# Six channel tiles of a gated convolution in pairs, seven block products in place of eight, and the latent q and k of two heads side by side

## The chip, the cores and the metric

The kernel runs on one core of one Trainium2 chip. The time is the device time of one execution in microseconds; before the change its median over three runs is 1995.36 us (1992.71 to 1997.35).

## What is computed

Two layers of a hybrid block over 256 context rows and 1024 latent rows of width 1024, all in float32. The change is in the first layer's input projection; its outputs are:

```
p = h @ w_in                                  # h: 1280 rows x 1024
q, k, v, g_a, a_f, a_b, c_b, c_c, c_x, g_b = split(p)
# 4 heads of gated linear attention: q, k 128 wide, v 256 wide, chunks of 64 rows, both directions
b = cumsum(log_gate)                          # per chunk
scores = (q * exp(b)) @ (k * exp(-b)).T       # masked; o = scores @ v + q_in @ state
o = rmsnorm(o_f + o_b) * silu(g_a)            # g_a: 8 tiles of 128 channels
# 8 channel tiles of 128 of the short convolution
z = c_c * c_x
y = c_b * conv3(z) * silu(g_b)                # conv3 within grid rows of 64 latents, or within the context
x = x + gate * (concat(o, y) @ w_out)
```

The second layer is a gated linear recurrence over 16 blocks of 128 channels with its own projections, and a final norm follows.

## The kernel before, in words

**Products.** h stands transposed in SBUF, 8 row blocks (k) of 128 by 1280 columns, as a high and a low float32r part (`hhi`, `hlo`). A weight unit of 128 output channels is two loads of 128x512 (`load_unit`, L115); each load goes through `load_split` (L104): a DMA into one of two `raw` buffers, a cast to the high part on ScalarE (L111), a subtraction for the low part on VectorE (L112) into one of six `hl` buffers. `mm3` (L123) makes one product of three matmuls (L125 to L127), and `proj` (L144) runs 8 of them for each column chunk of `CH`: 256 context columns and twice 512 latent columns. A unit is so 24 matmuls of 256 columns and 48 of 512.

**Stages.** A start stage norms h and projects q and k of head 0. Then for each of four heads: `emit_gla(h)` (L527), two gate units (L560, L562), four batches of `presplit` (L165), one convolution tile (`emit_conv`, L195, four units: cc, cx, cb and a gate), and q, k, v of the next head. `presplit` loads 128x512 weights of the second layer, splits them and stores both parts in DRAM for later. Behind the heads come convolution tiles 4 to 7, the modulation vectors (`mod`, L576: 32 loads of 512 KB and 56 reductions on VectorE, L586), the first output projection, the recurrence blocks and the last output projection.

**What sets the order.** From the heads to the first output projection the instructions are put in order by a scheduler, which takes the program's order as priority and fills each engine when an instruction's inputs are ready by its own timeline; the recurrence has a fixed order. Each engine runs its list in that order. Buffers bound it: two `raw`, six `hl`, and in PSUM three banks of tag A (projections), three of tag G (attention) and two of tag B (transposes).

**The attention's chain.** For one chunk `emit_gate` (L405) makes a matmul `pz` (L411), from it ScalarE and VectorE make the gate b (L414 to L420, a scan at the end), `emit_factors` (L423) makes from b, q and k the factors `qh`, `kh` (L456, L459), and `emit_scores` (L477) multiplies these: `psc` (L484 on). A chunk is called by head, direction (1 backward, 0 forward) and first column: `pz2_0_0` is head 2, forward, context. The buffers of q and k are one per chunk (L231), so the next head's projection can be copied out of PSUM when the factors of the present head are made.

## Time and profile before

| | |
|---|---|
| median of 3 runs | 1995.36 us |
| profiled execution, its own time | 2002.68 us |
| span of its trace | 2000.9 us |
| TensorE matmul (PE) busy | 1932.0 us, 97% |
| TensorE weight load (PEld) busy | 1588.5 us, 79% |
| VectorE (DVE) busy | 1317.8 us, 66% |
| ScalarE (ACT) busy | 961.3 us, 48% |

The profiled execution is 7.3 us over the median, 1.8 us of its time lie outside the span. Matmuls are pipelined, so that the busy time of one is longer than the distance from its start to the next start; the distance is what it costs. The heads run from about 120 to 830 us of the span, the convolution tiles 4 to 7 to about 990 us.

### The profile page before, as it was taken

The page shows a single profiled execution, that of the slowest core. Times are in us where ns is not written, and L with a number is a line of the kernel's source. Part 1 is how long each engine was busy: PE and PEld are TensorE (multiplying, and loading weights), DVE is VectorE, ACT ScalarE, POOL GpSimd, SP SyncE. Part 2 cuts the span into 40 slices and gives each one's busy share as a digit, 9 for nine tenths or more (in the row PEclk, how much of TensorE's full clock was granted, in tenths as well). Part 3 has the DMA queues.
Part 4 walks back from the last instruction along what each step waited for, and adds up shares of the span by engine and source line. Part 5 has one row for each costly group of instructions (what it writes and reads, how often), then busy time and mean ns, then how long its engine had stood idle before and what let it go on. Part 6 is the DMA issues. An engine that isn't in the chain of part 4 may idle for free.

```text
span 2000.9 us, 27096 instructions
## 1 busy us (share of the span) xinstructions
PE 1932.0 (97%) x9884; PEld 1588.5 (79%) x9884; DVE 1317.8 (66%) x2103; ACT 961.3 (48%) x1690; POOL 105.2 (5%) x154
## 2 busy tenths in 40 slices
PE   9899999999999999999999899999999999998988
PEld 5777898888788888888776678878888888876767
DVE  6746436543552554388557474689999999996595
ACT  4333344334433433311345444267777776876452
POOL 1000000000000000000000000201111010100000
PEclk9999999999999999999999999999999999999999
DMA  9256217514721751366655665434333343324782
GB/s 357 82 195 199 78 50 252 175 43 146 244 89 33 245 192 53 124 223 197 205 175 178 209 222 173 139 111 127 120 118 120 115 121 121 116 81 156 264 290 88
DMA packets 162522, 311.45 MB, mean 156 GB/s; under 512 B 16338, under 2 KB 37202, under 8 KB 162260
## 3 DMA queue, kind: packets, MB, share of 16 engines
q1 hardware_dynamic: 140628, 267.78, 40.1%
q0 software_dynamic: 21760, 41.95, 7.5%
q8 instruction: 77, 1.26, 0.3%
q14 instruction: 57, 0.47, 0.1%
HBM read 221.05 MB, written 88.60 MB: 155 GB/s over the span
## 4 chain that ended last, share of the span: by engine, by line
PE 60%; DMA 19%; DVE 12%; ACT 5%; issue 4%; SPq 1%; POOL 0%; DVEq 0%; ACTq 0%; POOLq 0%
PE pjgt L126 4%; PE pjgt L127 4%; PE pjgt L125 4%; DMA rawpre<-in_w1f 4%; PE pjxr L125 4%; PE pjxr L127 4%; PE pjxr L126 4%; PE pO L126 3%; PE pO L125 3%; PE pO L127 3%; PE po L515 2%; DMA wt<-in_wmT 2%; DMA rawo<-in_w0out 2%; PE pv L125 2%; PE pv L126 2%
## 5 line engine op out<-in xcount | busy, mean ns | idle before, releaser
L125 PE MATMUL pjgt<-hhi,wgt 128*128 128x512 f32 (+1 forms) x640 | 240.6, 376 | 6.0 <-DVE zc L218 6.0
L125 PE MATMUL pO<-wo,yh 128*128 128x512 f32 x576 | 224.2, 405 | 17.6 <-ACT wo L111 16.6
L126 PE MATMUL pjgt<-hlo,wgt 128*128 128x512 f32 (+1 forms) x640 | 240.5, 376 | 0.0
L127 PE MATMUL pjgt<-hhi,wgt 128*128 128x512 f32 (+1 forms) x640 | 239.5, 376 | 0.0
L126 PE MATMUL pO<-wo,yh 128*128 128x512 f32 x576 | 231.1, 402 | 7.2 <-DVE wo L112 7.2
L127 PE MATMUL pO<-wo,yl 128*128 128x512 f32 x576 | 228.5, 399 | 0.0
L806 DVE SCALAR_TENSOR_TENSOR xc<-xp,col,xc 128x1283 f32<-128x1283 f32 (+2 forms) x102 | 149.8, 1476 | 3.2
L111 ACT CAST wo<-rawo 128x512 fp32r<-128x512 f32 x160 | 98.0, 619 | 110.7 <-DMA rawo<-in_w0out 74.9
L112 DVE TENSOR_TENSOR wo<-rawo,wo 128x512 fp32r<-128x512 f32 x160 | 108.5, 687 | 63.6 <-ACT wo L111 63.0
L125 PEld LDWEIGHTS pO<-wo,yh 128*128 128x128 f32 x576 | 109.3, 191 | 50.0 <-ACT wo L111 22.5
L125 PEld LDWEIGHTS pjgt<-hhi,wgt 128*128 128x128 f32 x640 | 121.0, 189 | 30.1 <-DVE zc L218 6.6
L126 PEld LDWEIGHTS pjgt<-hlo,wgt 128*128 128x128 f32 x640 | 121.1, 189 | 23.7 <-issue 1.1
L127 PEld LDWEIGHTS pjgt<-hhi,wgt 128*128 128x128 f32 x640 | 120.5, 189 | 23.4 <-issue 0.7
L126 PEld LDWEIGHTS pO<-wo,yh 128*128 128x128 f32 x576 | 109.7, 190 | 36.8 <-DVE wo L112 12.4
L125 PE MATMUL pjxr<-hhi,wxr 128*128 128x512 f32 (+1 forms) x384 | 137.4, 359 | 0.0
L126 PE MATMUL pjxr<-hlo,wxr 128*128 128x512 f32 (+1 forms) x384 | 137.1, 358 | 0.0
L127 PE MATMUL pjxr<-hhi,wxr 128*128 128x512 f32 (+1 forms) x384 | 136.8, 358 | 0.0
L127 PEld LDWEIGHTS pO<-wo,yl 128*128 128x128 f32 x576 | 109.8, 191 | 24.6 <-DVE yl L685 0.3
L112 DVE TENSOR_TENSOR wpre<-rawpre,wpre 128x512 fp32r<-128x512 f32 x80 | 55.1, 690 | 90.1 <-ACT wpre L111 89.7
L125 PE MATMUL pv<-wv,hhi 128*128 128x256 f32 (+1 forms) x320 | 91.8, 287 | 2.4 <-ACT v L387 2.4
L127 PE MATMUL pv<-wv,hlo 128*128 128x256 f32 (+1 forms) x320 | 92.9, 290 | 0.0
L126 PE MATMUL pv<-wv,hhi 128*128 128x256 f32 (+1 forms) x320 | 92.8, 290 | 0.0
(270 smaller groups left out, 4527.9 us busy)
## 6 DMA issues: line engine op xcount, KB each, us to landing
w1s_d<-wpre SPq DMA_DIRECT2D x160, 256.0 KB, 2.6
rawo<-in_w0out SPq DMA_DIRECT2D x96, 256.0 KB, 3.2
rawpre<-in_w1f SPq DMA_DIRECT2D x64, 256.0 KB, 3.1
wt<-in_wmT SPq DMA_DIRECT2D x32, 512.0 KB, 4.3
rawo<-in_w1out SPq DMA_DIRECT2D x64, 256.0 KB, 3.3
wxr<-w1s_d POOLq DMA_DIRECT2D x32, 512.0 KB, 3.8
wgt<-w1s_d POOLq DMA_DIRECT2D x32, 512.0 KB, 3.8
wm<-in_wmT SPq DMA_DIRECT2D x24, 512.0 KB, 8.1
```

The costliest lines, as they stand in the source:

```text
L111: S.copy(hi, raw)
L112: V.tensor_tensor(lo, raw, hi.bitcast(F32), ALU.subtract)
L125: PE.matmul(ps, a[0], b[0], start=first, stop=False)
L126: PE.matmul(ps, a[0], b[1], start=False, stop=False)
L127: PE.matmul(ps, a[1], b[0], start=False, stop=last)
L515: PE.matmul(ps[:, :DV], l, r, start=(i == 0), stop=(i == len(pairs) - 1))
L806: V.scalar_tensor_tensor(x, tap(j), cw[j], x, op0=ALU.mult, op1=ALU.add)
```

## The change

The latents of convolution tiles 0, 1, 2, 4, 5, 6 leave the loop over heads and the plain tiles; they are computed in three pairs (0, 4), (1, 5), (2, 6), each quantity (cc, cx, cb, gate) of a pair by seven products of half blocks. A pair of units is a 256 x 1024 weight block A (halves of the channels by halves of k) against h as halves of k by halves of the latents; sums and differences of the blocks of h are made once (`make_t`), those of A for each job (`pair`), and seven products of 4 `mm3` of 512 columns stand for eight. The context columns of all eight tiles stay in the loop over heads, two tiles a head, and the split parts of the paired tiles' weights are stored in DRAM there. Tiles 3 and 7 stay plain. h is held in a context tile `hC` and a latent tile `hL`. q and k of the next head move right behind `emit_gla(h)`; odd heads have their own buffers for latent q and for the last latent k chunk.

```diff
+    hC = [hpool.tile([P, KD, NCTX], F32R, name=f"hC{i}") for i in range(2)]
+    hL = [hpool.tile([P, KD, NLAT], F32R, name=f"hL{i}") for i in range(2)]
...
+            if i < len(save) and save[i] is not None:
+                for j, part in enumerate((hi, lo)):
+                    SY.dma_start(save[i][:, j], part.bitcast(F32))
...
         def new_qk(kind, d, h, c0, n):
-            t = ap.tile([P, n], F32, tag=f"{kind}{c0}", name=f"{kind}{h}_{c0}")
+            pool = odd[0] if h % 2 and (kind, c0) != ("k", 256) and c0 else ap
+            t = pool.tile([P, n], F32, tag=f"{kind}{c0}", name=f"{kind}{h}_{c0}")
...
             for h in range(H):
                 emit_gla(h)
-                emit_raw_gate(w0f[8 + 2 * h], 2 * h)
-                presplit(5)
-                emit_raw_gate(w0f[9 + 2 * h], 2 * h + 1)
-                presplit(5)
-                for _ in emit_conv(h):
+                if h + 1 < H:
+                    emit_qk(h + 1)
+                for i in (2 * h, 2 * h + 1):
+                    emit_raw_gate(8 + i, i)
+                    presplit(5)
+                    run(emit_conv(i, CH[0]))
                     presplit(5)
                 if h + 1 < H:
-                    emit_qk(h + 1)
                     emit_v(h + 1)
-    for ct in range(H, KD - 1):
-        run(emit_conv(ct))
-    run(emit_conv(KD - 1, CH[:2]))
+    def make_t(tp):
...
+        for k in range(4):
+            def raw(kk, c0):
...
+                V.tensor_tensor(r, hi.bitcast(F32), lo.bitcast(F32), ALU.add)
+                return r
+            b11, b12, b22, b21 = raw(k, 256), raw(k, 768), raw(4 + k, 768), raw(4 + k, 256)
+            V.tensor_tensor(b11, b12, b11, ALU.subtract)
+            V.tensor_tensor(b12, b22, b12, ALU.subtract)
+            V.tensor_tensor(b22, b22, b11, ALU.subtract)
+            V.tensor_tensor(b21, b21, b22, ALU.subtract)
...
+                S.copy(dst[0], r)
+                V.tensor_tensor(dst[1], r, dst[0].bitcast(F32), ALU.subtract)
...
+    def pair(tp, T, units, nm, put):
...
+        a11 = saved(0, 0)
+        r11, r21, r22, r12 = raw(0, 0), raw(1, 0), raw(1, 1), raw(0, 1)
+        p = product("A", a11, block(0, 256))
+        S.copy(x1, p)
+        V.tensor_tensor(r21, r11, r21, ALU.subtract)
+        V.tensor_tensor(r22, r22, r21, ALU.subtract)
+        s2 = parts(r22, "s2")
+        a12 = saved(0, 1)
+        p = product("A", s2, comb(2))
...
+        put(0, 0, product("G", a12, block(4, 256)), x1, x1)
+        s3 = parts(r21, "s3")
+        p5 = product("G", s1, comb(1))
...
+        put(0, 1, product("G", s4, block(4, 768)), u4, u4)
...
+    run(emit_conv(3, CH[2]))
+    T_ = make_t(tp)
+    for ct in (3, KD - 1):
+        run(emit_conv(ct, CH[1]))
...
+    for units, nm, put, around in jobs:
...
+        pair(tp, T_, units, nm, put)
...
+    rest = emit_conv(KD - 1, CH[2], "B")
```

How the order changes is shown at three places. The first is TensorE at the forward context chunk of head 2. Before, `pz2_0_0` stands within a convolution product (`pjcx2`), and 83 other matmuls follow before its scores `psc2_0_0`; the rows are those around `pz2_0_0`.

```order
L125 MATMUL pjcx2_768_5663<-hhi_84,wcx2_0_1_5608 128x512
L126 MATMUL pjcx2_768_5663<-hlo_85,wcx2_0_1_5608 128x512
L411 MATMUL pz2_0_0_4876<-aT_843,wst_837 128x256
L127 MATMUL pjcx2_768_5663<-hhi_84,wcx2_0_1_5608 128x512
L125 MATMUL pjcx2_768_5663<-hhi_84,wcx2_0_1_5608 128x512
L126 MATMUL pjcx2_768_5663<-hlo_85,wcx2_0_1_5608 128x512
```

Of the changed kernel, the same engine and chunk:

```order
L527 MATMUL pst2_1_5_4790<-v2_5_4500,k1T2_1_256_4772 128x256
L527 MATMUL pst2_1_4_4794<-v2_4_4473,k1T2_1_256_4772 128x256
L527 MATMUL pst2_1_3_4798<-v2_3_4446,k1T2_1_256_4772 128x256
L434 MATMUL pz2_0_0_4804<-aT_847,wst_841 128x256
L507 MATMUL psc2_0_0_4843<-qh2_0_0_4823,kh2_0_0_4824 64x128
L508 MATMUL psc2_0_0_4843<-qh2_0_0_4823,kh2_0_0_4824 64x64
L507 MATMUL psc2_0_0_4843<-qh2_0_0_4823,kh2_0_0_4824 64x128
L508 MATMUL psc2_0_0_4843<-qh2_0_0_4823,kh2_0_0_4824 64x64
L128 MATMUL pjgt4_0_5373<-hC0_84,wgt4_0_0_5365 128x256
```

The scores now stand right behind `pz2_0_0`, and the next projection (`pjgt4`, a gate unit) behind the scores. The four heads read alike here.

The second place is VectorE at the weights of the next head's v. Before, the splits `wv3` (L112) stand beside the forward chunks of head 2:

```order
L495 COPY_PREDICATED Cs_844<-msk_76,psc2_0_0_4915 64x256
L496 COPY_PREDICATED Cs_844<-msk_76,psc2_0_0_4915 64x2x64
L498 COPY_PREDICATED Ds_846<-msk_76,psc2_0_0_4915 64x2x64 x2
L499 TENSOR_TENSOR Cs_844<-Cs_844,Ds_846 128x256
L88 TENSOR_SCALAR rvo2_0_4931<-sso2_0_4929 128x1
L88 TENSOR_SCALAR rvo2_1_4952<-sso2_1_4950 128x1
L509 SCALAR_TENSOR_TENSOR S0_2_1_4965<-S0_2_0_4944,dec2_0_0_4890,pst2_0_1_4963 128x256
L415 TENSOR_SCALAR b2_2_0_256_4968<-pz2_0_256_4969,col_74 128x512
L112 TENSOR_TENSOR wv3_0_6131<-rawv3_0_6129,wv3_0_6131 128x512
```

Of the changed kernel, VectorE from the first scores of head 3 on:

```order
L515 COPY_PREDICATED Cs_848<-msk_76,psc3_1_0_6342 64x256
L516 COPY_PREDICATED Cs_848<-msk_76,psc3_1_0_6342 64x2x64
L112 TENSOR_TENSOR wpre11_1_5985<-rawpre11_1_5983,wpre11_1_5985 128x512
L112 TENSOR_TENSOR wpre11_2_5992<-rawpre11_2_5990,wpre11_2_5992 128x512
L112 TENSOR_TENSOR wpre11_3_5999<-rawpre11_3_5997,wpre11_3_5999 128x512
L112 TENSOR_TENSOR wpre11_4_6006<-rawpre11_4_6004,wpre11_4_6006 128x512
L112 TENSOR_TENSOR wv3_0_6013<-rawv3_0_6011,wv3_0_6013 128x512
```

From `wcb4_0_0`, the first split beside head 2's forward chunk at column 256, to `wv3_0` there are 30 splits in a row of the same two raw buffers: 12 of convolution units for the context columns, 2 of a gate unit, 15 of `presplit`, and `wv3_0` itself. In the list of TensorE the 216 matmuls of 256 columns, 48 of 512, 24 output products (`po`, L515 before) and 55 smaller ones stand between the first use of tile 4's weights and the first `pv3`.

The third place is VectorE where the plain tiles end. Before, beside tile 5, the reductions (L586, an `ISA` row each) and a small computation (L609, L610) are in the list with that tile's product of z:

```order
L205 TENSOR_TENSOR z5_0_8052<-pjcx5_0_8152,z5_0_8052 128x256
L609 TENSOR_TENSOR l_pl_9219<-l_pl_9219,l_s2_9218 128x32
L610 TENSOR_SCALAR l_pl_9219<-l_pl_9219 128x32
L586 ISA junk0_9053,modc_9050<-wt0_9051,crb_9047 128x1024
L586 ISA modc_9050 128x1
L609 TENSOR_TENSOR l_pl_9219<-l_pl_9219,l_s2_9218 128x32
```

Of the changed kernel, VectorE beside tile 3's latents; `b0_256` and the like are the sums of h's parts, `T2`, `T3`, the second halves of `hL1` and `hC1` the low parts of the combined blocks:

```order
L611 TENSOR_TENSOR b4_768_7679<-b4_768_7679,b0_256_7675 128x512
L748 ISA junk0_9744,modc_9741<-wt0_9742,crb_9738 128x1024
L748 ISA modc_9741 128x1
L768 TENSOR_TENSOR l_s2_9909<-l_s_9908 128x32
L112 TENSOR_TENSOR wcx7_256_0_7947<-rawcx7_256_0_7945,wcx7_256_0_7947 128x512
L219 SCALAR_TENSOR_TENSOR zc3_256_7756<-z3_256_7755,col_74,zc3_256_7756 128x8x63
L616 TENSOR_TENSOR T3_1_7672<-b0_768_7677,T3_0_7671 128x512
L612 TENSOR_TENSOR b4_256_7681<-b4_256_7681,b4_768_7679 128x512
L605 TENSOR_TENSOR b1_256_7695<-hL0_86,hL1_87 128x512
L616 TENSOR_TENSOR T2_1_7670<-b4_768_7679,T2_0_7669 128x512
```

The reductions stand between the steps of `make_t` here. From `b0_256` to the low part of the first job's second product (`scc0s2`) VectorE has 64 operations of two 128x512 tensors, 17 reductions, 4 products-and-sums of 504 elements, 2 products of 512 with a scalar and 23 of at most 32 elements; beside them TensorE has 168 matmuls of 512 columns.

## Rows read from the trace of the kernel before

**Rows 1.** The page, its first lines: busy time (share of the span) and instructions.

```profile
span 2000.9 us, 27096 instructions
...
PE 1932.0 (97%) x9884; PEld 1588.5 (79%) x9884; DVE 1317.8 (66%) x2103; ACT 961.3 (48%) x1690; POOL 105.2 (5%) x154
```

**Rows 2.** Windows: PE, PEld, DVE, ACT, POOL busy, PEclk, DMA share, GB/s.

```profile
300.00:350.00 50.00, 49.69 (x267) 40.27 (x267) 30.34 (x65) 24.49 (x57) 0.00 (x0) 1.00 0.75 251
400.00:450.00 50.00, 49.04 (x301) 42.05 (x301) 20.84 (x48) 18.69 (x49) 2.19 (x4) 1.00 0.15 45
850.00:900.00 50.00, 50.00 (x252) 41.95 (x251) 40.70 (x77) 8.33 (x15) 0.00 (x0) 1.00 0.68 226
```

**Rows 3.** Timeline of PE, matmuls of 512 columns: start, us, operation.

```profile
835.14 0.40 PE L126 MATMUL pjcc<-hlo,wcc 128*128 128x512 f32 x1
...
837.94 0.40 PE L126 MATMUL pjcc<-hlo,wcc 128*128 128x512 f32 x1
```

**Rows 4.** Timelines of ACT and DVE: gate and factors of a 256-column chunk.

```profile
123.74 0.48 ACT L414 ACTIVATE b<-pz,col 128x256 f32<-128x256 f32 x1
...
128.81 0.42 DVE L456 TENSOR_TENSOR kh<-kh,k 128x256 f32<-128x256 f32 x1
```

**Rows 5.** The same of a 512-column chunk.

```profile
394.94 0.69 ACT L414 ACTIVATE b<-pz,col 128x512 f32<-128x512 f32 x1
...
401.47 0.68 DVE L459 TENSOR_TENSOR qh<-qh,q 128x512 f32<-128x512 f32 x1
402.07 0.68 DVE L456 TENSOR_TENSOR kh<-kh,k 128x512 f32<-128x512 f32 x1
```

**Rows 6.** Timeline of ACT, weight casts: entries 1, 13, 18, 25, 30.

```profile
486.04 0.62 ACT L111 CAST wpre<-rawpre 128x512 fp32r<-128x512 f32 x1 [1.15 <-DMA rawpre<-in_w1f]
...
516.32 0.62 ACT L111 CAST wpre<-rawpre 128x512 fp32r<-128x512 f32 x1 [0.71 <-DMA rawpre<-in_w1f]
...
531.19 0.62 ACT L111 CAST wcb<-rawcb 128x512 fp32r<-128x512 f32 x1 [2.79 <-issue]
...
549.27 0.62 ACT L111 CAST wgt<-rawgt 128x512 fp32r<-128x512 f32 x1 [1.17 <-DMA rawgt<-in_w0f]
...
561.19 0.62 ACT L111 CAST wk<-rawk 128x512 fp32r<-128x512 f32 x1 [1.49 <-DMA rawk<-in_w0f]
```

**Rows 7.** Timeline of PE, matmuls of 256 columns.

```profile
830.39 0.28 PE L125 MATMUL pjcc<-hhi,wcc 128*128 128x256 f32 x1
...
831.82 0.28 PE L125 MATMUL pjcc<-hhi,wcc 128*128 128x256 f32 x1
```

**Rows 8.** Timeline of PE, the attention's output products.

```profile
415.57 0.59 PE L515 MATMUL po<-v,Cs 128*128 128x256 f32 x2
416.00 0.59 PE L515 MATMUL po<-S,qb 128*128 128x256 f32 x2
```

**Rows 9.** Timeline of DVE, two reductions in a row.

```profile
879.24 1.23 DVE L586 CUSTOM_DVE_ANT_0 junk<-wt,crb 128x1024 bf16<-128x1024 f32 x1 [1.90 <-DMA wt<-in_wmT]
...
880.50 1.23 DVE L586 CUSTOM_DVE_ANT_0 junk<-wt,crb 128x1024 bf16<-128x1024 f32 x1
```

**Rows 10.** Lines of DVE: group, count | busy, mean ns | idle before.

```profile
L206 DVE TENSOR_SCALAR zc<-z,col 128x512 f32<-128x512 f32 x1 | 0.5, 487 | 0.0
L212 DVE SCALAR_TENSOR_TENSOR zc<-z,col,zc 128x504 f32<-128x504 f32 x2 | 1.5, 742 | 0.0
L609 DVE TENSOR_TENSOR l_pl<-l_pl,l_s 128x32 f32<-128x32 f32 x7 | 1.3, 189 | 0.1
```

**Rows 11.** Timeline of PE behind an idle time.

```profile
977.08 0.79 PE L125 MATMUL pjgt<-hhi,wgt 128*128 128x512 f32 x1 [4.32 <-DVE zc L218]
977.67 0.63 PE L126 MATMUL pjgt<-hlo,wgt 128*128 128x512 f32 x1
...
982.37 0.55 PE L125 MATMUL pjgt<-hhi,wgt 128*128 128x512 f32 x1
982.75 0.39 PE L126 MATMUL pjgt<-hlo,wgt 128*128 128x512 f32 x1
```

More of the change, by code (lines that the diff above doesn't have):

```diff
@@ L158, in hybrid_kernel, with kept @@
     g1_d = dram.tile([NB, P, NLAT], F32, name="g1_d")
+    PAIRED = (0, 1, 2, 4, 5, 6)
+    w0s_d = dram.tile([48, 2, P, 2, 512], F32, name="w0s_d")
+    def kept(u, c0):
+        ct = (u - 16) // 4
+        if c0 or ct not in PAIRED:
+            return ()
+        return (w0s_d[u, 0] if ct < 4 else None, w0s_d[u, 1])
+    b12_d = dram.tile([2, P, 4, 512], F32, name="b12_d")
     w1s_d = dram.tile([5 * NB, P, 2, 512], F32, name="w1s_d")
@@ new lines, in emit_conv @@
+    def emit_conv(ct, chunk, tag="A"):
+        c0, n = chunk
+        nm = f"{ct}_{c0}"
+        z = vp.tile([P, 512], F32, tag="z", name=f"z{nm}")[:, :n]
+        zc = vp.tile([P, 512], F32, tag="zc", name=f"zc{nm}")[:, :n]
+        for ps, _, _ in proj(load_unit(w0f[16 + 4 * ct], f"cc{nm}", kept(16 + 4 * ct, c0)), f"cc{ct}", [chunk], tag):
+            S.copy(z, ps)
+        for ps, _, _ in proj(load_unit(w0f[17 + 4 * ct], f"cx{nm}", kept(17 + 4 * ct, c0)), f"cx{ct}", [chunk], tag):
+            V.tensor_tensor(z, ps, z, ALU.mult)
+        short_conv(ct, zc, z, NCTX if c0 == 0 else 64)
@@ L216, in emit_conv @@
         yield
[L217 to L219 removed]
+        for ps, _, _ in proj(load_unit(w0f[18 + 4 * ct], f"cb{nm}", kept(18 + 4 * ct, c0)), f"cb{ct}", [chunk], tag):
+            V.tensor_tensor(zc, ps, zc, ALU.mult)
+        SY.dma_start(y0_d[ct, :, c0:c0 + n], zc)
         yield
[L221 removed]
+        emit_raw_gate(19 + 4 * ct, 8 + ct, [chunk], tag)
@@ L352, in hybrid_kernel @@
         with sbuf("gla") as gp:
+            odd.append(gp)
             def gt(shape, tag, name, bufs=1, dt=F32):
@@ new lines, in put_z, with put_mul, put_y, start @@
+    def put_z(ct, half, ps, add, out):
+        V.tensor_tensor(half_of(zs[ct], half), ps, add, ALU.add)
+    def put_mul(t, half, ps, add, out):
+        V.tensor_tensor(out, ps, add, ALU.add)
+        V.tensor_tensor(half_of(t, half), out, half_of(t, half), ALU.mult)
+    def put_y(ct, half, ps, add, out):
+        put_mul(zcs[ct], half, ps, add, out)
+        SY.dma_start(y0_d[ct, :, NCTX + 512 * half:NCTX + 512 * half + 512], half_of(zcs[ct], half))
+    jobs = []
+    for ct in range(3):
+        c = (ct, ct + 4)
+        def start(c=c):
+            for i in c:
+                zt(zs, i)
+        def conv(c=c):
+            for i in c:
+                short_conv(i, zt(zcs, i), zs[i], 64)
+        fs = [lambda r, *a, c=c: put_z(c[r], *a), lambda r, *a, c=c: put_mul(zs[c[r]], *a),
+              lambda r, *a, c=c: put_y(c[r], *a), lambda r, *a, c=c: put_gate0(8 + c[r], *a)]
+        for j, nm in enumerate(("cc", "cx", "cb", "gb")):
+            o = 16 + j
+            jobs.append(((o + 4 * c[0], o + 4 * c[1]), f"{nm}{ct}", fs[j],
+                         (start, None) if j == 0 else (None, conv) if j == 1 else None))
@@ L576, in hybrid_kernel @@
+    for units, nm, put, around in jobs:
+        before, after = around or (None, None)
+        if before:
+            before()
+        pair(tp, T_, units, nm, put)
+        if after:
+            after()
+    for i in range(2):
+        G.dma_start(hL[i][:, 0:4, 512:], b12_d[i])
+    rest = emit_conv(KD - 1, CH[2], "B")
     with sbuf("mod") as mp:
```

106 lines of the change are left out of this document (74 added, 32 removed).

## The prediction

> **What bounds the kernel now.** I read the page first. TensorE's matmuls are busy 97% of the span, VectorE 66%, ScalarE 48% [rows 1]. The windows, read next, tell that this holds stage by stage: in three stretches of 50 us, two within the heads and one in the plain convolution tiles, PE is idle at most 1 us, the granted clock is 1.00, and the DMA share swings between 0.15 and 0.75 without showing in PE [rows 2]. So in the part that the change touches the kernel is bound by the number of matmul columns, and everything else is covered. This is what a saving of matmuls needs, and also what makes the kernel sensitive: a wait comes into the time as soon as TensorE has nothing to put into it.
>
> The third view is the timeline of PE, for the price of a column. Twelve matmuls of 512 columns start 2.80 us apart, 0.2333 us each [rows 3]; twelve of 256 take 1.43 us, 0.119 each [rows 7]. The last views are ACT's and DVE's timelines, for the prices of what PE may have to wait for: the attention's chain [rows 4, 5], the loads [rows 6], VectorE's operations [rows 9, 10], and PE's clock behind a pause [rows 11].
>
> **Part 1, the seven products.** 12 jobs have 84 matmuls of 512 columns where the plain form has 96: 144 fewer. The list of TensorE has exactly so many rows less (9161 for 9305). At 0.2333 us that is **-33.6 us** [rows 3]. The context columns cost the same matmuls as before. The Trainium skill ("TensorE: Matmul & The Clock Gate", section "Wait — 56ns, not 53.3ns?") gives 215.7 ns from start to start for 512 columns on a warm array; the row has 233.3, and the measurement decides. By the page's figure the saving would be 31.1 us.
>
> **Part 2, the attention's chain without cover.** Before, 83 other matmuls stand between `pz2_0_0` and its scores, so ScalarE's and VectorE's chain from gate to factors is hidden. In the changed list nothing stands between. The reason is in the banks: q and k of the next head are projected early, their context parts share buffers with the present head, so their three results wait in the three A banks until this very chunk's factors are made, and no further projection can start. The chain is paid in full. From the gate's first step (123.74) to the second factor's end (128.81 + 0.42) it takes 5.5 us [rows 4], and with 0.4 us from the matmul to the gate and the hand-over to the scores 6.0. I take 6.0 in each of four heads: **+24**. Below, if VectorE reorders nothing and part of the chain overlaps the last state products in front, 4 us; above, with weight splits of 0.69 us in VectorE's list between the steps, 8.
>
> Head 0 has two more such places, the two latent forward chunks, where the list has 2.6 and 0.3 us of matmuls behind `pz`. A chain of 512 columns takes from 394.94 to 402.75, 7.8 us [rows 5], with the lead 8.2. That is 8.2 - 2.6 + 8.2 - 0.3 = **+13.5**.
>
> **Part 3, loads in a row.** In the heads weights go through two raw buffers. In a stretch of the trace with nothing but such splits, 30 casts follow each other between 486.04 and 561.19: 29 distances in 75.15 us, 2.59 each, and ACT waits for the DMA at each row shown but one [rows 6]. The slowest part, with the stores of `presplit` between (516.32 to 531.19, 5 distances), has 2.97 each, the fastest without stores (549.27 to 561.19, 5) 2.38. Before, this was covered, since a convolution tile's 8 splits fed 192 matmuls of 512 columns; now the same 8 splits feed 96 matmuls of 256. In the changed list 30 splits stand between the first weight of tile 4's last units and the first of the next head's v, and PE has beside them 216 x 0.119 + 48 x 0.2333 + 24 output products x 0.43 [rows 3, 7, 8] = 47.2 us, and 55 smaller ones that I estimate at 0.16 us, 9: 56.2 us together. The splits before this are no help, since the six `hl` buffers are full while PE is in the backward chunks. With two of the 30 loaded ahead the rest need 28 x 2.59 = 72.5 us: 16.3 us idle in each of three heads, **+49**. Bounds: nothing, if the loads run ahead of the place where I let them start (the spacing of rows 6 would then be hidden), and 28 x 2.97 - 56.2 = 27 us in each, +81, with the slow spacing; the stores for the six paired tiles are more of what slowed that stretch. I take the mean spacing, as it holds both kinds.
>
> **Part 4, the combined blocks.** `make_t` and the first sums of the weights are one chain on VectorE. From the first sum of parts to the low part of the first job's second product its list has 64 operations of 512 elements at 0.60 us from start to start [rows 5], 17 reductions at 1.26 [rows 9], 4 at 0.74, 2 at 0.49 [rows 10], and 23 small ones, some 2 us as they overlap: 38.4 + 21.4 + 3.0 + 1.0 + 2 = 66 us. PE has 168 matmuls of 512 columns beside them, 39.3 us [rows 3], and behind these the product that needs the last entry of VectorE's list. The reductions belong to `mod`, which is not needed yet, but they stand in the list between the sums and VectorE runs them there. PE waits 66 - 39 = **+27**. Below: the list starts while PE is still at head 3's end, so VectorE may be some 20 us early, +7; above: +35, if the first sums wait for the raw loads of the weights too. After this VectorE has 17 to 20 us of work to a job, PE 84 x 0.2333 = 19.6, and I count nothing. The context copies of ScalarE lie beside. At the far end, where the pairs give way to the first output projection, before has an idle time of 4.32 us of its own [rows 11], and I count no change.
>
> **Part 5, the clock.** Behind that 4.32 us of idle time PE's matmuls start 0.427 us apart from 977.67 to 982.37, and 0.234 again from 982.75 [rows 11]: the granted clock was at the lower of its two levels, 1.2 GHz for 2.4. Twelve matmuls at 0.427 - 0.234 = 0.193 more make 2.3 us. The chains of part 2 in four heads and the wait of part 4 are pauses as long or longer: 5 x 2.3 = **+11.5**. The Trainium skill (the same page, section "HAM oscillation — how this bites in real kernels") says that such a loss is paid again at each pause and not once in the kernel; the row shows one pause and agrees. By that rule the three waits of part 3 would pay too, 7 us more, if each is one long wait; I see them as many short ones and leave them out.
>
> **The sum.** -33.6 + 24 + 13.5 + 49 + 27 + 11.5 = +91. The profiled execution has 2002.7 us of its own, which gives 2094; it lies 7.3 us over the median of the runs, and in their terms the forecast is **2087 us**.
>
> **Rivals.**
>
> *The cover moves and does not go (faster).* The order is one of lists, and nothing in a list says when an instruction is ready. If loads and VectorE run far enough ahead, all of parts 3 and 4 is hidden and the chains cost only what the scores' own latency did before; then nearly the whole saving stays, -33.6 with up to 10 us of chains: 1970. For it speaks that PE is 97% busy and VectorE has 34% of the span free [rows 1]; against it that nothing stands between `pz` and `psc` in four heads, which no timing of other engines fills. It decides if PE's idle time at these four places stays under 2 us in sum each.
>
> *Loads keep up.* The heads have 48 splits each, 48 x 2.59 = 124 us, and PE some 142 us of work (an estimate from the counts of its list at the distances of [rows 3, 7, 8]). If the splits were spread as PE needs them, part 3 would be nothing, and what is left is -33.6 + 24 + 13.5 + 27 + 11.5 = +42: 2038. Against it stands that the six buffers bind the loads to PE's progress.
>
> *Loads are slower.* With 2.97 us to a split, as beside the stores, part 3 is +81 in place of +49: 2120. For it: the paired tiles' split parts are stored as well, through the same queue, ahead of the next load.
>
> *The change is worth nothing either way.* 33.6 us saved and as much lost, within 0.2% (4 us, about what a measurement of this kernel can tell from no change). No mechanism ties the two, so it gets what chance leaves.
>
> **How the numbers follow.** The forecast has 0.50, loads that keep up 0.22, slower loads 0.13, cover that moves 0.11, no difference 0.04. The first three are slower than before, 0.85, of which 0.01 goes to a far end of loads that keep up with all the lower bounds, which comes out faster: slower 0.84, the same 0.04, faster 0.12. The range leaves out the fast rival and the far ends of the bounds: from 2010 (loads that keep up, with part 4 at its lower bound of 20 less and the 4 us chain in the four heads, 2038 - 20 - 8) to 2130 (slower loads and VectorE's upper bound, 2120 + 8, rounded).
>
> **What would show it.** In the changed profile PE should have idle times of about 6 us at each `pz` of a head's forward context chunk, released by ACT or DVE and not by a DMA, and two of some 6 to 8 us more in head 0. Before the first `pv` of heads 1 to 3 PE's idle times should be released by L111 or L112, 16 us in sum, with ACT's own idle time there put down to the DMA of `rawpre`, `rawcc` and the like. Before the second product of the first job one wait of some 27 us on VectorE should stand, with reductions in VectorE's timeline beside it. The granted clock should fall at each. A head should take about 160 us, and each of the twelve jobs 20. The forecast is wrong if PE's idle time in the heads is under 10 us (loads keep up), if VectorE's list begins so early that the second product is not late, or if a job takes more than 23 us, as VectorE would then set the pace of the pairs.

## The result, and the profile after

The changed kernel takes 2143.56 us (median of 4 runs, 2135.00 to 2145.16) against 1996.36 us of the kernel before on the same chip (1992.71 to 1998.42): a ratio of 1.0731, 95% interval 1.0698 to 1.0764. It is slower, as forecast, but by 147 us and not by 91; 2143.56 lies above the stated range.

The first view is the page of the changed kernel, its busy times (answers to [rows 1]).

```profile
span 2143.4 us, 27691 instructions
...
PE 1943.5 (91%) x9740; PEld 1589.3 (74%) x9740; DVE 1474.3 (69%) x2366; ACT 1003.9 (47%) x1766; POOL 132.9 (6%) x192
```

TensorE has 144 instructions less and is 6 points of busy share down; its wait is the loss. Where the loss lies is read from the first and last start of three groups in the kernel before (median duration in ns, then first and last start): the attention's first `pz`, the first matmul of the first output projection, the first of the recurrence.

```profile
L411 PE MATMUL pz<-aT,wst x24: 379/498/503, 123.3 to 789.8; 64*128 64x512 f32 x16, 64*128 64x256 f32 x8
L125 PE MATMUL pO<-wo,yh x576: 387/394/797, 985.7 to 1993.0; 128*128 128x512 f32 x192
L125 PE MATMUL pjxr<-hhi,wxr x384: 276/395/502, 1266.7 to 1753.8; 128*128 128x512 f32 x129, 128*128 128x256 f32 x63
```

The same groups of the changed kernel:

```profile
L434 PE MATMUL pz<-aT,wst x24: 378/498/579, 125.4 to 769.6; 64*128 64x512 f32 x16, 64*128 64x256 f32 x8
L128 PE MATMUL pO<-wo,yh x576: 387/394/796, 1127.7 to 2135.6; 128*128 128x512 f32 x192
L128 PE MATMUL pjxr<-hC,wxr x128: 277/281/364, 1408.9 to 1883.6; 128*128 128x256 f32 x128
```

From the first `pz` to the output projection it took 862.4 us and takes 1002.4: 140.0 of the 142.5 us that the span grew. Behind that, the output projection takes 281 us in both. So nearly all of it lies in the heads and the pairs. Windows of the changed kernel (columns as in [rows 2]) show both:

```profile
250.00:300.00 50.00, 32.22 (x224) 28.78 (x222) 18.01 (x41) 17.63 (x44) 1.18 (x2) 0.86 0.68 226
400.00:450.00 50.00, 42.54 (x247) 35.96 (x245) 26.52 (x55) 25.54 (x62) 3.47 (x6) 0.93 0.72 235
600.00:650.00 50.00, 31.58 (x197) 28.10 (x198) 21.45 (x48) 20.91 (x50) 2.20 (x4) 0.83 0.71 233
850.00:900.00 50.00, 24.41 (x96) 18.82 (x95) 49.42 (x98) 10.16 (x17) 2.15 (x3) 0.73 0.56 185
```

Where PE was idle at most 1 us of 50 [rows 2], it now lacks 7 to 18 in the heads, and 26 where the combined blocks are made, with VectorE full (49.42). PE's timeline names what ended the longest waits: the factors of the attention (L479), the weights of v (L111), the parts of the first job's weights (L635).

```profile
153.22 0.47 PE L511 MATMUL psc<-qh,kh 128*64 128x128 f32 x1 [7.39 <-DVE kh L479]
...
166.27 0.47 PE L511 MATMUL psc<-qh,kh 128*64 128x128 f32 x1 [6.94 <-DVE kh L479]
...
177.87 0.47 PE L507 MATMUL psc<-qh,kh 128*64 128x128 f32 x1 [4.47 <-DVE kh L479]
...
281.66 0.58 PE L128 MATMUL pv<-wv,hC 128*128 128x256 f32 x1 [13.40 <-ACT wv L111]
...
455.75 0.47 PE L511 MATMUL psc<-qh,kh 128*64 128x128 f32 x1 [9.26 <-DVE kh L479]
...
641.03 0.58 PE L128 MATMUL pv<-wv,hC 128*128 128x256 f32 x1 [12.63 <-ACT wv L111]
...
881.10 0.80 PE L128 MATMUL pcc<-T,scc0s 128*128 128x512 f32 x1 [24.31 <-ACT scc0s L635]
```

And the lines of PE by group (count | busy, mean ns | idle before, releaser):

```profile
L545 PE MATMUL pot<-ident,on 128*128 128x128 f32 x80 | 16.1, 283 | 8.3 <-ACT on L542 8.3
L511 PE MATMUL psc<-qh,kh 128*64 128x128 f32 x80 | 15.5, 339 | 28.1 <-DVE kh L479 28.1
L128 PE MATMUL pv<-wv,hC 128*128 128x256 f32 x48 | 14.0, 334 | 29.4 <-ACT wv L111 29.4
L507 PE MATMUL psc<-qh,kh 128*64 128x128 f32 x80 | 13.2, 310 | 20.1 <-DVE kh L479 20.1
```

In the kernel before, the two groups of scores wait 0.8 and 0.1 us in sum, `pot` and the weights of v not at all.

I summed PE's timeline from the first `pz` to the first `pO` in both kernels: idle time as the profile marks it, and for the rest the distance from start to start against a price for the operation (0.2333 us for 512 columns, 0.119 for 256, for the attention's own operations the third decile over both kernels). The parts, in us:

| from the first `pz` to the first `pO` | before | after | change | forecast |
|---|---|---|---|---|
| projections and products, at their price | 699.7 | 666.2 | -33.5 | -33.6 |
| attention, at its price | 109.7 | 109.7 | 0 | 0 |
| idle before the attention's matmuls | 3.9 | 67.1 | +63.2 | +37.5 |
| idle before projections and products | 13.1 | 83.0 | +69.9 | +76 |
| matmuls further apart than their price | 36.0 | 76.0 | +40.0 | +11.5 |
| sum of the rows | 862.4 | 1002.0 | +139.6 | +91.4 |

The stretch itself grew from 862.4 to 1002.4 us; 0.4 us of the second are in no row. The prices are a choice: with slightly other ones the first row comes to -34.4 and the last to +41.3. The granted clock over the two stretches (the last column but two; before, then after) goes with the last row:

```profile
123.32:985.66 862.34, 845.32 (x4763) 713.96 (x4763) 455.44 (x958) 317.93 (x748) 21.90 (x40) 0.99 0.47 153
```

```profile
125.36:1127.75 1002.39, 851.56 (x4633) 710.40 (x4632) 610.45 (x1220) 357.30 (x817) 49.66 (x78) 0.92 0.58 189
```

### The profile page after: what moved, and what is told of

It reads as the page before. It is cut to its first block, busy times and chain, and to the rows that moved or that the text cites. A ratio compares the mean times of both kernels' runs of the same rounds, so it can differ in the third digit from the quotient of the medians.

```text
span 2143.4 us, 27691 instructions
## 1 busy us (share of the span) xinstructions
PE 1943.5 (91%) x9740; PEld 1589.3 (74%) x9740; DVE 1474.3 (69%) x2366; ACT 1003.9 (47%) x1766; POOL 132.9 (6%) x192
## 4 chain that ended last, share of the span: by engine, by line
PE 58%; DMA 19%; DVE 11%; ACT 6%; issue 4%; SPq 1%; POOL 0%; DVEq 0%; ACTq 0%; POOLq 0%
PE pjgt L128 4%; PE pjgt L129 4%; PE pjgt L130 4%; PE pjxr L130 3%; PE pjxr L128 3%; PE pjxr L129 3%; DMA rawpre<-in_w1f 3%; PE pO L128 3%; PE pO L129 3%; PE pO L130 3%; DMA y<-y_d 2%; DMA rawo<-in_w0out 2%; DMA rawpre<-in_w1ax 2%; PE pg L129 2%; PE pg L128 2%
## 5 line engine op out<-in xcount | busy, mean ns | idle before, releaser
L128 PE MATMUL pO<-wo,yh 128*128 128x512 f32 x576 | 227.6, 410 | 18.1 <-ACT wo L111 13.7
L129 PE MATMUL pO<-wo,yh 128*128 128x512 f32 x576 | 235.2, 409 | 8.3 <-DVE wo L112 7.9
L128 PE MATMUL pjgt<-hL,wgt 128*128 128x512 f32 x416 | 166.6, 400 | 0.0
L129 PE MATMUL pjgt<-hL,wgt 128*128 128x512 f32 x416 | 165.8, 398 | 0.0
L130 PE MATMUL pjgt<-hL,wgt 128*128 128x512 f32 x416 | 165.1, 399 | 0.0
L111 ACT CAST wo<-rawo 128x512 fp32r<-128x512 f32 x160 | 98.1, 619 | 122.4 <-DMA rawo<-in_w0out 69.0
L128 PEld LDWEIGHTS pO<-wo,yh 128*128 128x128 f32 x576 | 111.6, 195 | 51.1 <-ACT wo L111 19.4
L112 DVE TENSOR_TENSOR wo<-rawo,wo 128x512 fp32r<-128x512 f32 x160 | 108.8, 688 | 49.3 <-ACT wo L111 48.8
L129 PEld LDWEIGHTS pO<-wo,yh 128*128 128x128 f32 x576 | 112.0, 194 | 39.1 <-DVE wo L112 14.3
L112 DVE TENSOR_TENSOR wpre<-rawpre,wpre 128x512 fp32r<-128x512 f32 x80 | 55.2, 690 | 94.7 <-ACT wpre L111 94.4
L128 PE MATMUL pjxr<-hL,wxr 128*128 128x512 f32 x256 | 101.5, 397 | 0.0
L129 PE MATMUL pjxr<-hL,wxr 128*128 128x512 f32 x256 | 101.0, 396 | 0.0
L130 PE MATMUL pjxr<-hL,wxr 128*128 128x512 f32 x256 | 100.8, 396 | 0.0
L111 ACT CAST wpre<-rawpre 128x512 fp32r<-128x512 f32 x80 | 49.5, 619 | 92.4 <-DMA rawpre<-in_w1f 53.3
L129 PEld LDWEIGHTS pjgt<-hL,wgt 128*128 128x128 f32 x416 | 79.0, 190 | 18.3
L128 PEld LDWEIGHTS pjgt<-hL,wgt 128*128 128x128 f32 x416 | 79.0, 190 | 18.1 <-issue 0.2
L130 PEld LDWEIGHTS pjgt<-hL,wgt 128*128 128x128 f32 x416 | 78.1, 188 | 18.8 <-issue 0.9
L845 DVE TENSOR_TENSOR y<-y,ga 128x512 f32<-128x512 f32 (+1 forms) x56 | 36.4, 650 | 63.8 <-DMA y<-y_d 60.2
L832 ACT ACTIVATE ga<-ga 128x512 f32<-128x512 f32 (+1 forms) x80 | 47.0, 588 | 70.1 <-DMA ga<-gt_d 48.2
```

The costliest lines, as they stand in the source:

```text
L111: S.copy(hi, raw)
L112: V.tensor_tensor(lo, raw, hi.bitcast(F32), ALU.subtract)
L128: PE.matmul(ps, a[0], b[0], start=first, stop=False)
L129: PE.matmul(ps, a[0], b[1], start=False, stop=False)
L130: PE.matmul(ps, a[1], b[0], start=False, stop=last)
L832: silu = S.activation(ga, ga, AF.Silu)
```

## The experiments

All are compared with 2143.56 us (the changed kernel) and the kernel before, which ran beside each (medians of 1991.4 to 1994.5). Idle times are of the profiled execution.

Small differences need care. Beside the changed kernel the kernel before took 1996.36 us, so up to 5 us of a difference from 2143.56 need not be the edit's; the ratios are free of that. And the heads alone differ from execution to execution: the changed kernel, experiment 3 and experiment 5 run the same instructions in the same order up to the last transpose of the attention (`pot`), but from the first `pz` (125.4, 123.8 and 124.8 us) to the last `pot` they took 690.6, 686.2 and 681.5 us (lines in this order):

```profile
L545 PE MATMUL pot<-ident,on x80: 270/272/476, 191.3 to 815.9; 128*128 128x128 f32 x80
```

```profile
L545 PE MATMUL pot<-ident,on x80: 270/273/476, 189.4 to 810.0; 128*128 128x128 f32 x80
```

```profile
L545 PE MATMUL pot<-ident,on x80: 270/273/476, 191.6 to 806.4; 128*128 128x128 f32 x80
```

**1. q and k of the next head back in their old place.**

```diff
                 emit_gla(h)
-                if h + 1 < H:
-                    emit_qk(h + 1)
...
                 if h + 1 < H:
+                    emit_qk(h + 1)
                     emit_v(h + 1)
```

> The changed kernel with the next head's q and k projected behind the gates and context units again (where before had them); the buffers of odd heads stay. In TensorE's list 47 to 56 matmuls then stand between pz and psc of every head's forward context chunk, where the changed kernel has none; the backward chunk at column 256 keeps its gap in three heads. Theory A (missing cover: of the 107 us of idle time that the heads gained, 48 wait for the chain, L479, and the lower clock of some 39 us follows from the pauses): the chain's idle time falls to 10 to 20 us, the clock's loss by about a third, the time to 2085 to 2105. Rival B (the loads are the limit of the heads whatever the order, 48 splits by 2.59 us and blocked buffers): the idle time moves to L111 and L112, the time stays above 2130.

Measured: 2123.05 us, ratio to before 1.0664 (1.0643 to 1.0685). Less than theory A's gain, more than the rival's. The places of the list that were filled wait no more, but the backward chunk at column 256 waits instead in every head, 32.0 us at four places of 7.7 to 8.6, and the wait for the combined blocks is longer:

```profile
336.06 0.48 PE L511 MATMUL psc<-qh,kh 128*64 128x128 f32 x1 [8.01 <-DVE kh L479]
...
860.26 0.79 PE L128 MATMUL pcc<-T,scc0s 128*128 128x512 f32 x1 [36.33 <-ACT scc0s L634]
```

The early q and k alone are not the cause: 39.2 of the chain's 48.2 us stay without it. There is less to put into the gaps: in this kernel 181 us of projections stand between `pz` and `psc` over all 24 chunks (278 in the kernel before, by the distances 0.2333 and 0.119 us), and at the four chunks that wait longest at most 1.2 us.

**2. Without the preparation of the second layer's weights.** The list of these weights is cut to the first block's five, and `load_parts` reads these for all blocks.

```diff
-    todo = [(b, j) for b in range(NB) for j in range(5)]
+    todo = [(0, j) for j in range(5)]
...
-        G.dma_start(hl, w1s_d[5 * b + j])
+        G.dma_start(hl, w1s_d[j])
```

> The changed kernel without 75 of the 80 loads, splits and stores that prepare the second layer's weights beside the heads (all blocks of the second layer read the first block's, so its numbers are not the reference's; its work is the same). Theory A: the idle time put down to L111 and L112 in the heads, 47 us, falls to under 10, with a third of the clock's loss; the chain's 48 us stay: 2075 to 2095. Rival B (loads are the root, and the chain waits because VectorE and ScalarE run splits in between): nearly all idle time of the heads goes, 2020 to 2040. Rival C (the chain is the root, and loads are late only because the buffers come free late): the time stays above 2125.

Measured: 2079.25 us, 1.0424 (1.0402 to 1.0446), theory A's number. No idle time of PE in the heads is put down to L111 any more (44.3 before the edit). The chain stays, and the wait for the combined blocks doubles, as everything else is earlier:

```profile
L511 PE MATMUL psc<-qh,kh 128*64 128x128 f32 x80 | 16.3, 343 | 27.9 <-DVE kh L479 27.9
L507 PE MATMUL psc<-qh,kh 128*64 128x128 f32 x80 | 13.5, 305 | 13.4 <-DVE kh L479 13.4
...
L128 PE MATMUL pcc<-T,scc0s 128*128 128x512 f32 x8 | 4.7, 582 | 56.4 <-ACT scc0s L635 56.4
```

So loads and chain are two causes, each with its own size.

**3. The reductions behind the first job's second product.** Its low part's subtraction is remembered as `first[0]`, and the first load of `mod` is ordered behind it.

```diff
+            d = SY.dma_start(wt, wmT[16 + i])
+            if i == 0:
+                tc.add_manual_dep(d.ins, first[0], mybir.DependencyInfo(
+                    mybir.DependencyClass.NoSync, mybir.DependencyReason.DATA), reason="load order")
```

> The changed kernel with the 32 modulation loads, and so the 56 reductions, held back until the low part of the first job's second product is in VectorE's list. Theory A: VectorE's 66 us before that product lose 17 x 1.26 = 21 us, the wait of 24.3 us falls to about 3 to 5, and the time to about 2120 with the clock. Rival: the reductions are needed before the first output projection's end and make VectorE the bound of the jobs (17 to 20 us of work to a job of 19.6), so that what is gained comes back there: 2138 to 2148.

Measured: 2122.08 us, 1.0653 (1.0632 to 1.0674): theory A's time, with a wait of 9.08 us where 3 to 5 were expected. Part of that is VectorE waiting 1.55 us for the raw weights near the end. From the last `pot` to the first `pO`, where the edit acts, the kernel takes 298.1 us for 311.8: 13.7 of the 21.5 us of the medians.

```profile
859.97 0.80 PE L128 MATMUL pcc<-T,scc0s 128*128 128x512 f32 x1 [9.08 <-ACT scc0s L637]
```

**4. The kernel before with early q and k alone.**

```diff
                 emit_gla(h)
+                if h + 1 < H:
+                    emit_qk(h + 1)
                 emit_raw_gate(w0f[8 + 2 * h], 2 * h)
...
                 if h + 1 < H:
-                    emit_qk(h + 1)
                     emit_v(h + 1)
```

> The kernel before with one thing changed: the projection of the next head's q and k directly behind the head's attention, with the shared buffers. Its list has no matmul between pz and psc in three chunks of heads 0 to 2 and six in a fourth, while all latents of the convolution stay in the heads. Theory A (the three A banks hold q and k that wait for the factors, so the chain is uncovered): 3 heads x (2 x 8.2 + 6.0 + 7.5) = 90 us of idle time released by L456, and 10 to 20 us of clock: 2085 to 2110. Rival (with the latents in the heads PE has other work that the list puts in front, so that the chain has begun early enough): within 10 us of before, 1996.

Measured: 2101.80 us, 1.0557 (1.0521 to 1.0593). Theory A: 77.5 us of waits for the chain where 90 were counted from the list, all work being that of before.

```profile
L488 PE MATMUL psc<-qh,kh 128*64 128x128 f32 x80 | 17.2, 371 | 46.8 <-DVE kh L456 46.8
L484 PE MATMUL psc<-qh,kh 128*64 128x128 f32 x80 | 16.1, 345 | 30.7 <-DVE kh L456 30.7
```

The latents were still in the heads and did not help, because the list has them behind the banks that wait. An order alone costs 109 us.

**5. Matmuls that serve nothing, in the wait for the combined blocks.**

```diff
                 T[j, k] = tuple(dst)
+                if k >= 2:
+                    ps = bank("B", f"pwarm{j}{k}")
+                    for i in range(8):
+                        PE.matmul(ps, dst[0][:, :P], dst[0], start=i == 0, stop=i == 7)
```

> The changed kernel with 64 matmuls of 512 columns added that serve nothing: eight behind each of the last eight combined blocks, so that TensorE, in its wait of 24.3 us for the first job's second product, has some 15 us of work in pieces as VectorE makes the blocks. Nothing on VectorE changes. Theory A (the 27 us at the lower of the clock's two levels around this wait follow from TensorE's pause, and the jobs behind it pay): the stretch at the lower level shrinks to under 10 us, the product waits about as long as before, the time is 5 to 9 us shorter, 2134 to 2139. Rival 1 (the clock there costs nothing because VectorE paces the first job anyway): no change, 2140 to 2147. Rival 2 (the added matmuls delay the product): 5 to 15 us longer.

Measured: 2135.30 us, 1.0726 (1.0707 to 1.0745). The median is 8.3 us under the changed kernel's, theory A's number, but the ratio is nearly the changed kernel's (1.0731). The clock does what theory A says: between 850 and 900 us it is 0.90 for 0.73 (the last shown window above), PE's long wait is cut in pieces, and the first matmul of the product behind it takes 0.50 us where it took 0.80.

```profile
850.00:900.00 50.00, 43.14 (x163) 33.75 (x164) 49.06 (x95) 8.96 (x15) 2.85 (x4) 0.90 0.61 195
```

```profile
851.88 5.35 PE L621 MATMUL pwarm<-T 128*128 128x512 f32 x16 [2.78 <-ACT T L615]
...
864.06 5.55 PE L621 MATMUL pwarm<-T 128*128 128x512 f32 x16 [3.20 <-ACT T L615]
...
871.47 0.50 PE L128 MATMUL pcc<-T,scc0s 128*128 128x512 f32 x1
...
873.97 0.50 PE L128 MATMUL pcc<-T,scc0s 128*128 128x512 f32 x1 [1.76 <-ACT scc0s L639]
```

But it saves no time at this place. VectorE's first sums start at 809.36 us here and at 818.89 in the changed kernel (first line here, second there), and the first output projection at 1118.3 and 1127.7:

```profile
809.36 2.49 DVE L605 TENSOR_TENSOR b<-hL,hL 128x512 f32<-128x512 f32 x4
```

```profile
818.89 2.49 DVE L605 TENSOR_TENSOR b<-hL,hL 128x512 f32<-128x512 f32 x4
```

```profile
L128 PE MATMUL pO<-wo,yh x576: 387/394/796, 1118.3 to 2124.8; 128*128 128x512 f32 x192
```

From the first sums to the product it is 62.1 us (62.2 in the changed kernel), and from there to the output projection 246.8 (246.6). So the gain is in the heads, which the edit does not touch; the fastest run of the changed kernel was 2135.00 as well. What was to be won here is small: with the product started, matmuls ran at the lower level from 881.1 to 886.7 us in the changed kernel, and here, where the clock falls once more, from 875.5 to 878.9. This is the first rival: VectorE's list says when the product starts.

**6. The first and third edit together.** Nothing else is changed.

```diff
-                if h + 1 < H:
-                    emit_qk(h + 1)
                 for i in (2 * h, 2 * h + 1):
...
+            if i == 0:
+                tc.add_manual_dep(d.ins, first[0], mybir.DependencyInfo(
```

> The two edits of the first and third experiment together: the next head's q and k behind the gates and context units, and the modulation loads behind the first job's second product. Alone they took 20.5 and 21.5 us off 2143.6. Theory A (they stand at different places, and the first made the second wait longer, 37.6 us for 25.6): the two add up or more, 2085 to 2102. Rival (the wait for the combined blocks swallows what the heads gain, since VectorE reaches it no earlier): 2115 to 2123.

Measured: 2106.96 us, 1.0584 (1.0566 to 1.0602), between the two expectations and 5 us above theory A's. Of the medians it is 36.6 of the 42 us that the two gave alone; in the ratios, which allow for the kernel beside, the two add up: 0.0067 and 0.0078 less alone, 0.0147 together. They act at different places; the wait at the combined blocks is 20.50 us, where the first experiment had 36.33 and the third 9.08.

**7. The heads as before, one pair behind them.** `emit_conv` takes lists of chunks again, and the loop is the old one with context units added; q and k have their old order and buffers again.

```diff
+                emit_raw_gate(8 + 2 * h, 2 * h)
+                presplit(5)
+                emit_raw_gate(9 + 2 * h, 2 * h + 1)
+                presplit(5)
+                for _ in emit_conv(h, CH):
+                    presplit(5)
+                if h in CTXH:
+                    run(emit_conv(CTXH[h], [CH[0]]))
+                if h + 1 < H:
+                    emit_qk(h + 1)
+                    emit_v(h + 1)
...
-    PAIRED = (0, 1, 2, 4, 5, 6)
+    PAIRED = (4, 5)
+    CTXH = {1: 4, 2: 5, 3: 7}
...
-    run(emit_conv(3, CH[2]))
+    run(emit_conv(6, [CH[0], CH[2]]))
     T_ = make_t(tp)
-    for ct in (3, KD - 1):
-        run(emit_conv(ct, CH[1]))
+    for ct in (6, KD - 1):
+        run(emit_conv(ct, [CH[1]]))
```

> The heads as they were before the change (each with a whole convolution tile, q and k where they were, buffers shared), with the context columns of tiles 4, 5 and 7 added behind heads 1 to 3, and behind the heads only one pair, (4, 5), by seven products; tile 6 and the first latent half of tile 7 stay plain, the latter beside the combined blocks. 48 matmuls of 512 columns fewer than before: -11.2 us. TensorE's list has 32 to 76 matmuls between pz and psc at each chunk. Theory A (the products' saving is real and was lost to missing cover): the heads lose under 10 us to waits, the attention's part of the loss is gone, the wait for the combined blocks stays some 20 us with the reductions before it: 1990 to 2010. Rival B (seven products lose by themselves, by VectorE's sums and the clock): 2015 or more. Rival C (everything hidden): 1983 to 1987.

Measured: 2039.47 us, 1.0236 (1.0214 to 1.0259): rival B's side of the expectation. The heads are healed, as theory A has it: 11.5 us of idle time in all where the changed kernel has 117.9, and 1.4 and 0.8 us at the two groups of scores. The loss of 48 us against before is behind them, on VectorE:

```profile
915.38 0.80 PE L128 MATMUL pcc<-T,scc4s 128*128 128x512 f32 x1 [25.48 <-ACT scc4s L642]
...
1011.67 0.79 PE L128 MATMUL pO<-wo,yh 128*128 128x512 f32 x1 [15.96 <-ACT yh L855]
...
1031.46 0.55 PE L797 MATMUL pggate<-dggate,ones 128*128 128x128 f32 x1 [9.44 <-DVE dggate L796]
```

```profile
900.00:950.00 50.00, 33.34 (x129) 26.29 (x130) 48.82 (x93) 8.34 (x14) 3.57 (x5) 0.77 0.63 200
```

VectorE is busy 48.82 of 50 us (third busy column), and PE waits. Before, it already had 40.70 in such a window [rows 2]: the plain tiles hide the 70 us of reductions (56 at 1.26 us [rows 9]), and there is too little room for the sums of a pair.

**8. The same with the reductions held back.** The edit of experiment 3 on the kernel of experiment 7.

```diff
+            if i == 0:
+                tc.add_manual_dep(d.ins, first[0], mybir.DependencyInfo(
```

> The one-pair kernel with the modulation loads held back behind the first job's second product. Theory A: VectorE's list before that product has no reductions left, 44 us of work beside 45 us of TensorE's, and the wait falls to 0 to 5 us; the saving of 11.2 us shows less the clock and the join: 1983 to 1993, faster than before by 3 to 12 us. Rival B (the reductions, 70 us, now fall on the four jobs and the first output projection, whose splits share VectorE): 1993 to 2005.

Measured: 2050.10 us, 1.0295 (1.0274 to 1.0316), later than both expectations. The reductions come back at the gate of the output projection, which needs their sums; of the two places where VectorE's list is late, one is traded for the other.

```profile
895.12 0.80 PE L128 MATMUL pcc<-T,scc4s 128*128 128x512 f32 x1 [9.44 <-ACT scc4s L644]
...
988.70 0.80 PE L128 MATMUL pO<-wo,yh 128*128 128x512 f32 x1 [15.78 <-ACT yh L862]
...
1043.27 0.55 PE L804 MATMUL pggate<-dggate,ones 128*128 128x128 f32 x1 [43.40 <-DVE dggate L803]
```

**9. The sums of the one-pair kernel on GpSimd.**

```diff
-                V.tensor_tensor(r, hi.bitcast(F32), lo.bitcast(F32), ALU.add)
+                G.tensor_tensor(r, hi.bitcast(F32), lo.bitcast(F32), ALU.add)
...
-            V.tensor_tensor(b11, b12, b11, ALU.subtract)
+            G.tensor_tensor(b11, b12, b11, ALU.subtract)
```

> The one-pair kernel (2039.5 us) with the sums and differences of make_t and of the jobs' weights moved from VectorE to GpSimd: 32 operations of 128x512 in make_t and 16 in the jobs. Theory A (all that is left over before is VectorE's backlog: 26.8 us at the combined blocks, 16 us at the first y and 11.7 us at the gate of the first output projection): VectorE has 19 us less before the second product and 10 less behind it, and GpSimd takes about as long for one, beside it: 2005 to 2020. Rival (GpSimd is slower for each and stands in the same chain, so that the wait for the combined blocks grows): 2040 to 2070. No row of this case shows such an operation on GpSimd.

Measured: 2060.83 us, 1.0330 (1.0307 to 1.0352), the rival: the wait for the combined blocks is 36.55 us, where the kernel of experiment 7 had 25.48.

```profile
931.81 0.80 PE L128 MATMUL pcc<-T,scc4s 128*128 128x512 f32 x1 [36.55 <-ACT scc4s L642]
```

One sum takes 1.80 us on GpSimd, where the kernel of experiment 7 had 0.68 on VectorE (lines, by group):

```profile
L612 POOL TENSOR_TENSOR b<-hL,hL 128x512 f32<-128x512 f32 x16 | 28.7, 1802 | 18.8 <-DVE hL L623 7.6 <-DVE T L623 5.3 <-PE pot L550 5.2
```

**10. And 24 reductions as products on GpSimd with sums on ScalarE.** Behind the heads the buffers of the convolution (`z`, `zc`) are also made anew, 768 columns wide in place of 1280; this is not tested by itself.

```diff
+                if s == 1:
+                    pr = mp.tile([P, D], F32, tag="pr", name=f"pr{i}")
+                    G.tensor_tensor(pr, wt, crb[:, s], ALU.mult)
+                    S.activation(pr, pr, AF.Identity, accum_out=modc[:, i, s:s + 1])
```

> The same with the 24 reductions for the context row taken from VectorE too: GpSimd multiplies 128x1024, ScalarE sums. VectorE has 30 us less again between 845 and 1040 us. Theory A: the backlog at the first y and at the gate goes, 1985 to 2005, the first version near or under before. Rival (GpSimd's list, with 24 products of 128x1024 between the sums of make_t and the jobs, becomes the bound): 2040 to 2080.

Measured: 2085.40 us, 1.0457 (1.0437 to 1.0476), the rival again and past its end. The wait for the combined blocks is 67.31 us, and in it GpSimd (fifth busy column) is busy 48.88 of 50 us:

```profile
962.14 0.80 PE L128 MATMUL pcc<-T,scc4s 128*128 128x512 f32 x1 [67.31 <-ACT scc4s L648]
```

```profile
900.00:950.00 50.00, 0.00 (x0) 0.00 (x0) 37.76 (x27) 14.14 (x24) 48.88 (x24) 0.50 0.29 94
```

No version that I ran beats the kernel before.

## Why the prediction was wrong

Two steps failed, parts 2 and 5: the attention's idle time and the matmuls further apart than their price came 25.7 and 28.5 us above their terms (table). The other waits came 6.1 below theirs, in part by luck.

**The saving** of part 1 came: the page has 144 matmuls less, and the table -33.5 us for -33.6. That the two agree to 0.1 us is luck, as other work crosses the first `pz` too: before, 50 matmuls of a gate unit (8.9 us) stand ahead of it, after, 47 of the next q (11.0 us). The twelve jobs run as reckoned: 996 matmuls between the second product's start (881.10) and the end of the last job at 1117.0 take 235.9 us, 0.237 each, so neither VectorE nor the loads set the pace of a job.

**The loads** of part 3 were sized well in sum, 49 us forecast. L111 and L112 released 47.1 us of idle time in the heads (44.3 and 2.8), less 4.7 of before; experiment 2 shows that it is the loads. The place differs: 16.3 us in each of three heads was forecast, and 13.4, 2.8 and 12.6 stand at v, the rest in small waits of gate and context units, some in head 3, which has no next v. So the sum is in part luck.

**The combined blocks** of part 4 were right: 27 us forecast, 24.31 and 1.28 measured. VectorE's list from 818.9 to 882.9 us takes 64 us, where the sum had 66. That the reductions in it cost some 15 us of the wait is shown by experiment 3.

**The first step that failed** is part 2, "The chain is paid in full ... I take 6.0 in each of four heads: +24", and head 0's +13.5. At the places named, the waits are near it or smaller: 4.47 or 4.48 us in heads 0 to 2, 6.68 in head 3, and 14.3 in the two of head 0 (which are its backward latent chunks; the prediction called them forward). What failed is that I took only these places, and only the first step of the attention behind them. Counted in TensorE's list, the projections between `pz` and `psc`, by 0.2333 and 0.119 us, are 278 us over the 24 chunks before, and no chunk has less than 7.1; in the changed list they are 162 us, and eight chunks have less than 3.4. One of these, head 2's backward context chunk, I had missed: 0 us between, and the longest wait of the chain, 9.26. And behind the chain come the state products, the output products and the transposes, which had other matmuls beside them before and now wait by themselves (`pot` alone 8.3). The attention's idle time grew by 63.2 us, 25.7 more than the sum had.

The reason that part 2 gives, early q and k that hold the banks, is only half of it. Four kernels have the two things in every combination, and their scores waited for `kh`: latents in the heads and q and k late 0.8 us (before), latents there and q and k early 77.5 (experiment 4), latents gone and q and k late 39.2 (experiment 1), both changes 48.2 (the changed kernel, whose odd heads have buffers of their own). Either change uncovers the chain. Experiment 7, which takes both back, brings all idle time in the heads to 11.5 us.

**The second step that failed** is the clock of part 5, mis-sized by about as much: 5 pauses at 2.3 us were 11.5, and matmuls that stand further apart than their price make 40.0 us, 16.2 of it on projections and 23.8 on the attention's own. Half the clock after a pause is a part of it: behind the wait at 281.66 the matmuls of 256 columns start 0.21 us apart for 4 us, and six state products at 169.96 take 2.9 us. There are not 5 such pauses but eleven of over 4 us (seven of the chain, two of the loads, one at the combined blocks, one at the gate of the output projection), where before has two, and shorter ones. The rule of the Trainium skill that I weighed and left out for the loads ("TensorE: Matmul & The Clock Gate", section "HAM oscillation — how this bites in real kernels", the loss is paid at each pause) is what this trace agrees with: the lower level was granted for 152 us of this stretch, and for 10 before. Sorted by the level that was granted at each matmul (in the count with the slightly other prices, +41 us), 18 us of the growth lie on projections at the lower level, 18 on the attention's own matmuls at the lower level, and 5 on the attention's at the full one. So most of this row is the clock; how much of the attention's 18 is still the latency of short matmuls that follow each other with nothing between stays open. The longest pause cost little of it: at the combined blocks 5.6 us of matmuls ran at the lower level, and filling that pause gained nothing (experiment 5).

**The range** ended at 2130, because its upper end took the worse of the loads but the same chain and the same clock: part 2's own upper bound of 8 us in each head was left out of it (with it, 2138), and the clock had no bound. The three signs of being wrong that the prediction lists did not come up either: they were for loads that keep up, a product that is not late and slow jobs, and none for more places where the attention waits.

## What to carry to other kernels

A kernel whose bound engine is at 97% has its other engines' latencies paid by the filler work in between; before moving that work elsewhere, count for each serial chain what is left beside it in the new list, all its steps and not only the first, in us and not in instructions. A cheaper product that is prepared on another engine needs room on that engine in the stage where it runs: here VectorE had 40.70 of 50 us before, and one pair that saves 11.2 us of TensorE's time lost 48.

## What the runs showed of the hardware

With GpSimd adding 128x512 tensors beside it, VectorE's own operations with two inputs in SBUF got slower. The low parts of T take 683 ns in experiment 7 and 867 in experiment 9, the 56 reductions 1218 and 1505 (lines of experiment 9):

```profile
L755 DVE CUSTOM_DVE_ANT_0 junk<-wt,crb 128x1024 bf16<-128x1024 f32 x56 | 84.3, 1505 | 3.9 <-DMA wt<-in_wmT 3.6
L623 DVE TENSOR_TENSOR T<-b,T 128x512 fp32r<-128x512 f32 x8 | 6.9, 867 | 0.0
```

In experiment 10, with more on GpSimd, the reductions that stay on VectorE take 2124:

```profile
L769 DVE CUSTOM_DVE_ANT_0 junk<-wt,crb 128x1024 bf16<-128x1024 f32 x32 | 68.0, 2124 | 17.6 <-DMA wt<-in_wmT 17.6
```

So moving 24 of 56 reductions gave VectorE nothing against experiment 7: 68.0 us for 32 where 68.2 were for 56. In experiment 9 the 24 reductions that ran while GpSimd had an addition under way took 1893 ns on average, the other 32 took 1214. VectorE's 128x512 operations with both inputs in SBUF took 1184 (22 of them) and 683 (51) in the same way, between 820 and 1080 us; those with one input from PSUM took 680 and 679. The Trainium skill ("SBUF — State Buffer", section "Who interferes with whom") says that an operation of VectorE with two inputs in SBUF contends with GpSimd's reads; these rows agree. The Trainium skill puts an addition on GpSimd at about twice VectorE's time ("GPSIMD Engine Reference", section "3.1 Elementwise — side-by-side cycle accounting"). Here the mean is 1802 to 684 ns, 2.6 times, with both engines at work; the six additions of experiment 9 beside which VectorE had no operation with two inputs in SBUF took 1380 ns, 2.0 times, which agrees.
